# v of branch B: its load placed 14 products ahead of its transposes and splits

## The chip, the cores and the metric

One core of a Trainium2 chip runs the whole kernel. The metric is the device time of one execution in microseconds (us). Three runs of the kernel before gave 1984.55, 1987.9 and 1991.54 us; their median is 1987.9 us.

Names of the engines: PE is TensorE (matmuls and transposes), DVE is VectorE, ACT is ScalarE, POOL is GpSimd, and SP is SyncE, which here only issues transfers. POOL issues transfers too.

## The reference

One layer of a bidirectional encoder over 1024 tokens of width 1024, all in float32:

```python
h = x + 1/2 * SwiGLU_1(RMSNorm(x))
u = RMSNorm(h)
qa, ka, va, qb, kb, vb, ga, gb = split(u @ w_in)       # 512,512,512, 512,128,128, 1024,1024 columns
ya = neighbourhood_attention_2d(qa, ka, va, rpb)       # branch A: 8 heads of 64
yb = windowed_gqa_sink(rope(qb), rope(kb), vb, sink)   # branch B: 8 heads, 2 key/value heads of 64
h = h + (sigmoid(ga) * (ya @ w_a) + sigmoid(gb) * (yb @ w_b)) @ w_out
h = h + 1/2 * SwiGLU_2(RMSNorm(h))
y = RMSNorm_final(h)
```

The change is about `vb`, the 128 columns of the projection that are the values of branch B. They must be ready when branch B's attention begins, after the projection.

## The kernel before

**Exact products in three passes.** Every float32 operand is split into a high part (a copy to the rounded type `F32R`, made by ACT, line L88) and a low part (the rest, a subtraction made by DVE, L89). `mm3` multiplies high by high, high by low and low by high (L140, L142, L144). A matmul of 128x128 by 128x512 thus costs three.

**The projection as Strassen products.** The projection `u @ w_in` is run by `products` with `store_z`. It takes four channel blocks of 128 columns at a time, a "group" of two pairs (`m` = 0 and 1), and forms each pair with seven products of half size, P1, P2, P5, P6, P7, P3 and P4. So a group has 14 products, and there are five groups, 0 to 4: 70 products. One product is 12 matmuls on PE (4 chunks by 3 passes). While a product runs, ACT and DVE prepare the left sides of the products up to 8 later (`prep`, tiles `ws`), and ACT and DVE take the results out of the PSUM banks into slots of `fa` (`store_z`, L627 and L630). POOL then sends these to memory: `z_d` for the raw channels, `zs_d` for ready-made high and low parts (tiles `hs`), `g_d` for gates. The weights come through SP, one 512 KB tile at a time (`fetch`, L265, tiles `raw` or `fx`).

**PSUM.** There are eight banks, four with tag `g` and four with tag `d`. A group holds two `g` banks (its W sums, from P1 to P4) and, in turn, two and two `d` banks.

**What hangs on the products.** After given products, `at_end` calls what stands in `hooks` for the number of products that are still to come. `rope` (five times, k = 0 to 4) reads a block of q or k of branch B back from `z_d` in two shapes (tiles x and y, both from the pool `xs` of two buffers; L648 and L651, on SP), combines them on DVE (L652 to L654) and sends the result to `zr_d` (L655, on POOL). `v_b` reads block 17, the raw `vb`, back from `z_d` into one `xs` tile (L660), transposes it on PE in eight pieces into two `g` banks (L664), and splits these into the two tiles `mix["vb"]` (ACT L88 and DVE L89, four each, 128x256). `q_b`, `k_b` and `keep_u` follow at the end of the last group.

The hook of `v_b` has the number `14 * (NG - 2) - 12`, which is 30 products to come: it is called after P3 (m = 1) of group 2. That is the place in the program's text. The place in an engine's queue is chosen by a scheduler, which sorts the instructions of all engines before the kernel is built and keeps to the data; each engine then runs its own queue strictly in that order. PE, DVE, ACT, POOL and SP therefore each have a row of their own, and an instruction that waits holds up all that stand behind it on the same engine.

Of the kernel before, what the change touches and what calls it, by code (L numbers as in the profile page):

```python
# [15 lines left out]
P = 128  # L16
# [20 lines left out]
def trunk_kernel(ctx, tc, x, n1, wg1, wu1, wd1, nm, win, rpb, sink, wa, wb, wo,  # L37
                 n2, wg2, wu2, wd2, nf, c_rope, c_mask_a, c_mask_b, out):
    nc = tc.nc
# [10 lines left out]
    def nm_(s):  # L50
        uid[0] += 1
        return f"{s}_{uid[0]}"
# [11 lines left out]
    def new_fx(k, dt=F32):  # L64
        fx[k] = main.tile([P, 1024], dt, tag=f"fx{k}", bufs=1, name=nm_("fx"))
        return fx[k]
# [8 lines left out]
    def bank(tag):  # L75
        return ps.tile([P, 512], F32, tag=tag, name=nm_(tag))
# [4 lines left out]
    def xs4():  # L81
        return main.tile([P, 1024], F32, tag="xs", bufs=2, name=nm_("xs"))
# [4 lines left out]
    def split(dst_hi, dst_lo, src, eng=None):  # L87
        nc.scalar.copy(dst_hi, src)  # L88
        (eng or nc.vector).tensor_tensor(dst_lo, src, f32v(dst_hi), op=ALU.subtract)  # L89
# [492 lines left out]
    z_d = dram.tile([GA, T], F32, name="z_d")  # L582
# [8 lines left out]
    mix = {}  # L591
# [3 lines left out]
    NG = len(groups)  # L595
# [44 lines left out]
    def rope(k):  # L640
# [13 lines left out]
        nc.vector.tensor_tensor(x, x, y, op=ALU.add)  # L654
        nc.gpsimd.dma_start(zr_d[k], x)  # L655

    def v_b():
        mix["vb"] = [new_fx(k, F32R).rearrange("p (t d) -> p t d", t=NTT) for k in (0, 1)]
        r = xs4()
        nc.sync.dma_start(r, z_d[17 * P:18 * P, :])  # L660
        for n in range(2):
            pt = bank("g")
            for i in range(4):
                nc.tensor.transpose(pt[:, i * P:(i + 1) * P], r[:, (4 * n + i) * P:(4 * n + i + 1) * P], ident)  # L664
            pt = pt.rearrange("p (b s d) -> p b s d", s=2, d=HD)
            for s in range(2):
                v = mix["vb"][s][:, 4 * n:4 * n + 4, :]
                split(v[:, :, :HD], v[:, :, HD:], pt[:, :, s, :])
# [64 lines left out]
    def hook(n, *f):  # L733
        hooks.setdefault(n, []).append(f)

    for c in range(4):
        hook(14 * (NG - 1) - 2 - 3 * c, rope, c)
    hook(14 * (NG - 2) - 2, rope, 4)
    hook(14 * (NG - 2) - 12, v_b)
    hook(7, q_b, 0)  # L740
    hook(6, k_b)
    hook(4, q_b, 1)
# [357 lines left out]
    for i, dc in enumerate(a_order):  # L1100
        r = nxt.pop(0)
# [99 lines left out]
```

## Time and profile before

| what | value |
|---|---|
| runs | 1984.55, 1987.9, 1991.54 us, median 1987.9 |
| profiled execution | span 1987.6 us from its first to its last instruction; no other time of it is given |
| PE busy | 1938.4 us, 98% of the span |
| DVE, ACT, POOL busy | 1439.8, 957.4, 422.0 us |
| mean granted clock of PE | 0.993 of full speed |
| first matmul of the projection's group 3 | starts at 798.91 us of the span |

In a timeline's row the first number is the start in us from the span's start, the second the duration; then come engine, line, operation, out<-in and the count. A bracket gives the idle time before it and what ended that. A matmul's duration there is longer than its share of the engine, since matmuls overlap: the pace is read from start to start. In a row of a table by stretches the columns are the stretch, its length, the busy time (and the number of instructions) of PE, of PE's weight loads, of DVE, ACT and POOL, and then the granted clock of PE, the share of the DMA engines and GB/s. In a table of waits the numbers are the time in all, how often, and the longest.

### The profile page before, as it was taken

How to read it: one execution, taken by the hardware profiler on the slowest of the kernel's cores; microseconds unless marked ns; L12 is line 12 of the kernel's file. 1: busy time of each engine (PE TensorE's matmuls, PEld its weight loads, DVE VectorE, ACT ScalarE, POOL GpSimd, SP SyncE). 2: the span in 40 equal slices, each digit the busy share in tenths (PEclk: the TensorE clock that was granted, in tenths of full speed). 3: DMA queues.
4: the chain of work that ended last, by engine and by line, in shares of the span. 5: the costliest groups of instructions: out<-in, count | busy, mean ns of one | idle time of the engine just before them, and what ended most of it. 6: DMA issues, size and time to landing. Idle time of an engine off the chain costs nothing.

```text
span 1987.6 us, 25701 instructions
## 1 busy us (share of the span) xinstructions
PE 1938.4 (98%) x8968; PEld 1612.7 (81%) x8968; DVE 1439.8 (72%) x2495; ACT 957.4 (48%) x1857; POOL 422.0 (21%) x474
## 2 busy tenths in 40 slices
PE   6999999999999999999999999998999999999998
PEld 5788888888888778788888888887888888888886
DVE  7866566558967677768889866999656656659864
ACT  7433333334446443468777873365333333344453
POOL 4101001002500533311112134513101100105100
PEclk9999999999999999999999999999999999999999
DMA  6423323367233469973357675544332342393341
GB/s 194 147 85 106 121 92 106 108 220 277 84 121 125 145 160 243 201 174 107 87 143 173 172 253 195 179 147 127 120 114 88 105 126 85 125 349 129 108 140 62
DMA packets 257217, 290.31 MB, mean 146 GB/s; under 512 B 46880, under 2 KB 187552, under 8 KB 257088
## 3 DMA queue, kind: packets, MB, share of 16 engines
q1 hardware_dynamic: 200576, 203.09, 32.8%
q0 software_dynamic: 56512, 85.58, 15.2%
q8 instruction: 71, 1.16, 0.2%
q14 instruction: 58, 0.48, 0.1%
HBM read 202.01 MB, written 86.70 MB: 145 GB/s over the span
## 4 chain that ended last, share of the span: by engine, by line
PE 82%; DVE 8%; issue 4%; DMA 3%; POOL 2%; ACT 2%; SPq 0%; POOLq 0%; DVEq 0%; ACTq 0%
PE g L140 16%; PE g L142 16%; PE g L144 16%; PE d L140 10%; PE d L142 10%; PE d L144 10%; PE d L991 2%; DVE ws L89 2%; DVE ar L89 1%; DMA xs<-z_d 1%; PE d L970 1%; PE d L971 1%; PE g L1010 1%; PE g L1005 1%; DVE ar L1116 1%
## 5 line engine op out<-in xcount | busy, mean ns | idle before, releaser
L140 PE MATMUL g<-ar,ws 128*128 128x512 f32 x1208 | 455.7, 398 | 9.2 <-ACT ar L88 3.5
L142 PE MATMUL g<-ar,ws 128*128 128x512 f32 x1208 | 448.6, 392 | 3.7 <-DVE ar L89 3.7
L144 PE MATMUL g<-ar,ws 128*128 128x512 f32 x1208 | 447.3, 392 | 2.1 <-DVE ws L89 2.0
L89 DVE TENSOR_TENSOR ws<-raw,ws 128x512 fp32r<-128x512 f32 (+1 forms) x335 | 249.5, 748 | 189.6 <-ACT ws L88 188.4
L88 ACT CAST ws<-raw 128x512 fp32r<-128x512 f32 (+1 forms) x337 | 213.3, 638 | 272.6 <-PE d L144 108.5
L142 PEld LDWEIGHTS g<-ar,ws 128*128 128x128 f32 x1208 | 228.4, 189 | 52.0 <-DVE ar L89 4.4
L144 PEld LDWEIGHTS g<-ar,ws 128*128 128x128 f32 x1208 | 228.3, 189 | 51.7 <-DVE ws L89 3.2
L140 PEld LDWEIGHTS g<-ar,ws 128*128 128x128 f32 x1208 | 223.0, 189 | 51.9 <-ACT ar L88 4.7
L140 PE MATMUL d<-ar,ws 128*128 128x512 f32 x656 | 254.3, 392 | 4.7 <-DVE ar L89 4.7
L142 PE MATMUL d<-ar,ws 128*128 128x512 f32 x656 | 254.2, 391 | 0.0
L144 PE MATMUL d<-ar,ws 128*128 128x512 f32 x656 | 254.0, 391 | 0.0
L347 POOL DMA_DIRECT2D hid<-fx x98 | 53.1, 542 | 501.1 <-DVE fx L374 364.6
L140 PEld LDWEIGHTS d<-ar,ws 128*128 128x128 f32 x656 | 124.1, 189 | 31.4 <-issue 5.5
L144 PEld LDWEIGHTS d<-ar,ws 128*128 128x128 f32 x656 | 124.1, 189 | 25.9
L142 PEld LDWEIGHTS d<-ar,ws 128*128 128x128 f32 x656 | 124.0, 189 | 25.9
L89 DVE TENSOR_TENSOR ws<-ar,ws 128x512 fp32r<-128x512 f32 x114 | 109.1, 964 | 6.7 <-ACT ws L88 6.7
L89 DVE TENSOR_TENSOR ws<-fa,ws 128x512 fp32r<-128x512 f32 x80 | 55.3, 691 | 63.5 <-ACT ws L88 63.1
L88 ACT CAST ar<-raw 128x512 fp32r<-128x512 f32 (+1 forms) x83 | 56.0, 679 | 93.1 <-PE g L142 51.1
L140 PE MATMUL g<-ws,ws 128*128 128x512 f32 x232 | 90.9, 392 | 0.0
L142 PE MATMUL g<-ws,ws 128*128 128x512 f32 x232 | 90.4, 390 | 0.0
L144 PE MATMUL g<-ws,ws 128*128 128x512 f32 x232 | 90.3, 389 | 0.0
L978 ACT ACTIVATE fa<-fa,nmx 128x385 f32<-128x385 f32 (+3 forms) x128 | 75.5, 591 | 26.9 <-DVE nmx L975 26.2
(222 smaller groups left out, 3588.3 us busy)
## 6 DMA issues: line engine op xcount, KB each, us to landing
raw<-hid SPq DMA_DIRECT2D x70, 512.0 KB
hid<-fx POOLq DMA_DIRECT2D x98, 256.0 KB, 2.4
raw<-in_ffn_w_up_dram SPq DMA_DIRECT2D x32, 512.0 KB
ar<-in_ffn_w_down_dram SPq DMA_DIRECT2D x32, 512.0 KB
raw<-in_ffn_w_gate_dram SPq DMA_DIRECT2D x28, 512.0 KB
hid<-fa POOLq DMA_DIRECT2D x56, 256.0 KB, 2.7
raw<-in_w_in_dram SPq DMA_DIRECT2D x27, 512.0 KB
ar<-zs_d POOLq DMA_DIRECT2D x48, 256.0 KB, 5.0
```

Of the source, the lines that this page charges most:

```text
L88: nc.scalar.copy(dst_hi, src)
L89: (eng or nc.vector).tensor_tensor(dst_lo, src, f32v(dst_hi), op=ALU.subtract)
L140: nc.tensor.matmul(b, lhs[0], r[0], start=first, stop=False, **kw)
L142: nc.tensor.matmul(b, lhs[0], r[1], start=False, stop=False, **kw)
L144: nc.tensor.matmul(b, lhs[1], r[0], start=False, stop=last, **kw)
L347: nc.gpsimd.dma_start(hid[PRODUCTS.index(p), i], src)
L970: nc.tensor.matmul(b[:, :nw], un["q"][s], un["kd"][s][:, k0 * P:k1 * P], start=True, stop=False)
L971: nc.tensor.matmul(b[:, :nw], un["q"][s], un["kl"][s][:, k0 * P:k1 * P], start=False, stop=True)
L978: nc.scalar.activation(pr, pr, AF.Exp, scale=-1.0, bias=nmx[:, s:s + 1], accum_out=ssum[:, s:s + 1])
L991: nc.tensor.transpose(pt[:, i * P:(i + 1) * P], un["pr"][s][:, i * P:(i + 1) * P], ident)
L1005: nc.tensor.matmul(o[:, s], un["v"][s][:, un["k0"] + i, :], un["p"][s][:, i], start=i == 0, stop=i == last)
L1010: nc.tensor.matmul(o, un["v"][0][:, un["k0"] + i, :], un["p"][k][:, i], start=i + k == 0, stop=i + k == last + 1)
```

## The change

`v_b` is cut in two. `v_b_load` takes the `xs` tile and issues the load; it is hooked at 34 products to come, after P6 (m = 1) of group 2, four products earlier than before. `v_b` keeps the transposes and splits; it is hooked at 20 products to come, after P6 (m = 1) of group 3, ten products later than before.

```diff
+    def v_b_load():
+        mix["vraw"] = xs4()
+        nc.sync.dma_start(mix["vraw"], z_d[17 * P:18 * P, :])
+
     def v_b():
         mix["vb"] = [new_fx(k, F32R).rearrange("p (t d) -> p t d", t=NTT) for k in (0, 1)]
-        r = xs4()
-        nc.sync.dma_start(r, z_d[17 * P:18 * P, :])
+        r = mix.pop("vraw")
         for n in range(2):
             pt = bank("g")
...
     hook(14 * (NG - 2) - 2, rope, 4)
-    hook(14 * (NG - 2) - 12, v_b)
+    hook(14 * (NG - 2) - 8, v_b_load)
+    hook(14 * (NG - 2) - 22, v_b)
```

In the changed kernel the load is L659 and the transposes are L667. What the scheduler makes of it shows in the rows of three engines. In the names, `ws` is a left side of a product, `ar` a right side, `g` and `d` are PSUM banks, `xs` is the tile with the raw values.

PE before, at the transposes. The bank `d_6040` is P5 (m = 1) of group 3, `g_5941` is P1 (m = 0) of group 3:

```order
L142 MATMUL d_6040<-ar_4770,ws_5897 128x512
L144 MATMUL d_6040<-ar_4770,ws_5897 128x512
L664 MATMUL g_5877<-ident,xs_5875 128x128 [waits DMAHW4_49]
L664 MATMUL g_5877<-ident,xs_5875 128x128 x3
L664 MATMUL g_5886<-ident,xs_5875 128x128 x4
L140 MATMUL g_5941<-ar_4405,ws_5771 128x512 [waits Activation_49]
L142 MATMUL g_5941<-ar_4405,ws_5771 128x512
```

PE now, at the transposes. The bank `g_5938` is P6 (m = 1) of group 3, `g_5921` is P7 (m = 0) of it:

```order
L142 MATMUL g_5938<-ar_4769,ws_5918 128x512
L144 MATMUL g_5938<-ar_4769,ws_5918 128x512
L667 MATMUL g_6070<-ident,xs_5787 128x128 [waits DMAHW4_49,PE_49]
L667 MATMUL g_6070<-ident,xs_5787 128x128 x3
L667 MATMUL g_6079<-ident,xs_5787 128x128 [waits PE_49]
L667 MATMUL g_6079<-ident,xs_5787 128x128 x3
L140 MATMUL g_5921<-ar_84,ws_5935 128x512 [waits Activation_49]
```

Before, 45 matmuls of group 3 (P2, P2, P5 and nine of P5's last twelve) stood between group 2 and the transposes, and P1 of group 3 behind them. Now group 3 runs in its usual order, and 96 of its matmuls (P1, P2, P5, P6, two each) stand ahead of the transposes.

SP before, at the load. L651 is the last part of rope 4's loads, L265 a weight tile of group 4, L95 the weights of the first gate:

```order
L651 DMA xs_5662<-z_d 32x1024 x2
L660 DMA xs_5875<-z_d 128x1024 [waits DMAHW1_49,DMAHW0_49,DMAHW2_49,DMASW3_49,DMAHW3_49,DMASW2_49,DVE_49]
L265 DMA raw_6088<-in_w_in_dram 128x8x128 [waits DVE_49,Pool_49]
L95 DMA xs_6473<-in_w_in_dram 128x8x128 [waits DMAHW6_49,DMASW3_49]
L265 DMA raw_6090<-in_w_in_dram 128x8x128 [waits DMAHW7_49,DVE_49]
```

SP now, at the load:

```order
L651 DMA xs_5662<-z_d 32x1024 x2
L659 DMA xs_5787<-z_d 128x1024 [waits DMAHW1_49,DMAHW0_49,DMAHW2_49,DMASW3_49,DMAHW3_49,DMASW2_49,DVE_49]
L265 DMA raw_6088<-in_w_in_dram 128x8x128 [waits DVE_49,Pool_49]
L95 DMA xs_6473<-in_w_in_dram 128x8x128 [waits DMAHW6_49,DMASW3_49]
L265 DMA raw_6090<-in_w_in_dram 128x8x128 [waits DMAHW7_49,DVE_49]
```

Nothing moved there: the load stands at the same place among SP's 551 rows, with the same waits, the last of them on DVE.

ACT before, at the splits of v (`fx_5873` and `fx_5874`):

```order
L88 CAST ws_5996<-raw_5765 128x512
L627 COPY fa<-d_6023 128x512
L88 CAST fx_5873<-g_5877 128x4x64
L88 CAST fx_5873<-g_5886 128x4x64
L88 CAST fx_5874<-g_5877 128x4x64
L88 CAST fx_5874<-g_5886 128x4x64
L627 COPY fa<-g_5941 128x512
```

ACT now, at the splits of v (`fx_6068` and `fx_6069`; `g_5921` and `g_5938` are the sums of P6 of group 3, `ws_6092` is the left side of group 4's second P1):

```order
L627 COPY fa<-g_5921 128x512
L88 CAST ws_6052<-fx_77 128x512
L627 COPY fa<-g_5938 128x512
L88 CAST fx_6068<-g_6070 128x4x64
L88 CAST ws_6092<-raw_6088 128x512
L88 CAST fx_6068<-g_6079 128x4x64
L88 CAST fx_6069<-g_6070 128x4x64
L88 CAST fx_6069<-g_6079 128x4x64
```

The splits moved back behind the copies of P6's sums. On DVE the four subtractions moved back in the same way, from ahead of the copy of group 3's first P2 to ahead of that of its first P7. The rows of POOL stand as they stood, and apart from the stretch shown (some 100 rows of PE, 14 of DVE, 20 of ACT) so do all others. In PSUM, the transposes used to take the two banks that group 1 had left, so that group 3 took over group 2's; now group 3 takes the banks that group 1 left, the transposes take over group 2's, and group 4 takes over those of the transposes.

## The prediction

> **What bounds the kernel now.** I read the page first, then PE's waits, then PE's timeline at the transposes, and last the chain of waits to see what they hang on. From the page:
>
> ```profile
> span 1987.6 us, 25701 instructions
> PE 1938.4 (98%) x8968; PEld 1612.7 (81%) x8968; DVE 1439.8 (72%) x2495; ACT 957.4 (48%) x1857; POOL 422.0 (21%) x474
> PE 82%; DVE 8%; issue 4%; DMA 3%; POOL 2%; ACT 2%; SPq 0%; POOLq 0%; DVEq 0%; ACTq 0%
> ```
>
> PE is busy for 98% of the span and carries 82% of the chain that ended last. So what counts is where PE stands still, and at which clock it runs. PE's waits from 800 to 890 us hold one row, and its timeline shows the place (798.91 is the first matmul of group 3):
>
> ```profile
> PE g L664 <- DMA xs<-z_d: 4.5, 1, 4.5
> ...
> 798.91 0.39 PE L140 MATMUL d<-ar,ws 128*128 128x512 f32 x1
> ...
> 808.88 0.39 PE L144 MATMUL d<-ar,ws 128*128 128x512 f32 x1
> 813.79 1.97 PE L664 MATMUL g<-ident,xs 128*128 128x128 f32 x8 [4.51 <-DMA xs<-z_d]
> 815.41 0.78 PE L140 MATMUL g<-ar,ws 128*128 128x512 f32 x1
> 815.98 0.63 PE L142 MATMUL g<-ar,ws 128*128 128x512 f32 x1
> ...
> 818.54 0.47 PE L142 MATMUL g<-ar,ws 128*128 128x512 f32 x1
> 818.85 0.40 PE L144 MATMUL g<-ar,ws 128*128 128x512 f32 x1
> ```
>
> The transposes wait for their load, and all matmuls of group 3 behind them wait too. From 798.91 to 808.88 there are 44 steps: the pace is 0.2266 us a matmul. From 815.98 to 818.54 six steps take 2.56 us, 0.427 each. The table by stretches says why (the number before the last two is the granted clock):
>
> ```profile
> 808.00:812.00 4.00, 1.27 (x6) 0.73 (x4) 3.01 (x4) 0.38 (x1) 0.55 (x1) 0.98 0.27 71
> 812.00:816.00 4.00, 2.21 (x10) 2.12 (x11) 0.42 (x1) 0.58 (x2) 0.00 (x0) 0.50 0.99 328
> 816.00:820.00 4.00, 4.00 (x13) 3.17 (x12) 1.18 (x3) 0.83 (x4) 0.00 (x0) 0.66 0.46 134
> 820.00:824.00 4.00, 4.00 (x19) 3.33 (x18) 2.66 (x5) 3.01 (x6) 1.61 (x2) 1.00 0.17 42
> ```
>
> The idle PE lost half its clock, and ran at half speed till about 818.5. So the stall has a tail.
>
> What the load waited for stands in the chain of waits, with SP's rows behind it:
>
> ```profile
> 795.15 5.23 DMA zr_d<-xs
> ...
> 807.36 1.24 DVE xs L653
> 808.62 1.24 DVE xs L654
> 809.87 3.87 DMA xs<-z_d
> ```
> ```profile
> 809.87 0.34 SPq L660 DMA_DIRECT2D xs<-z_d  x1
> 811.12 0.40 SPq L265 DMA_DIRECT2D raw<-in_w_in_dram  x1
> ```
>
> The load was not late because it was issued at its use. It needed an `xs` buffer, and that became free when rope 4's addition (L654) ended at 809.86; SP issued it at 809.87, and it landed at 813.74. In front of that stand rope 3's store and rope 4's loads, a chain that PE's pace does not set at this point.
>
> **The change part by part.** *The load.* SP's row is unchanged, and so is the buffer and its release by L654. Nothing ahead of it on SP, POOL or DVE moved. On ACT the two copies of P1's sums come in earlier (0.59 us each, as in the row at 799.53 below, from about 801.6 on), ahead of P7's left sides, whose low parts stand before L653 on DVE; but L653 starts only with its data, at 807.36. So I cost the earlier hook at nothing: the load is still issued at 809.87 and lands at 813.74.
>
> *The transposes.* This is what moves. Ahead of them stand now 96 matmuls of group 3 and not 45. If PE runs through from 798.91, their turn comes at 798.91 + 96 x 0.2266 = 820.66, which is 6.9 us after the landing. The wait goes. Their own cost without a stall is seen at eight others of the same shape amid a full stream:
>
> ```profile
> 611.27 0.39 PE L144 MATMUL g<-ws,ws 128*128 128x512 f32 x1
> 611.50 1.03 PE L133 MATMUL d<-ident,xs 128*128 128x128 f32 x8
> 612.29 0.48 PE L140 MATMUL g<-ws,ws 128*128 128x512 f32 x1
> 612.61 0.39 PE L142 MATMUL g<-ws,ws 128*128 128x512 f32 x1
> ```
>
> From 611.27 to 612.61 are two matmul steps (0.45) and the transposes: 1.34 - 0.45 = 0.89 us.
>
> *The sum on PE.* Before, from 808.88 to 818.85, 9.97 us pass. In it are nine matmul steps, 9 x 0.2266 = 2.04 us, and eight transposes, worth 0.89 us at full clock. What is left is 9.97 - 2.04 - 0.89 = 7.04 us. Of this 4.68 us are the standstill (808.88 + 0.23 to 813.79), and 2.36 us the slow clock behind it.
>
> [...]
>
> *Group 3 in its usual order.* P1 comes ahead of P2 and P5 now. Its banks are those of group 1, long read. Are the left sides ready?
>
> ```profile
> 794.76 0.69 DVE L89 TENSOR_TENSOR ws<-raw,ws 128x512 fp32r<-128x512 f32 x1
> ...
> 804.60 0.69 DVE L89 TENSOR_TENSOR ws<-raw,ws 128x512 fp32r<-128x512 f32 x1
> ```
>
> The first is P2's second left side; P1's two stand ahead of it on DVE, so P1 finds them at 798.91. The second is that of P6 (m = 1), needed at 798.91 + 84 x 0.2266 = 817.9: 12 us of slack. I cost this at nothing. The cover is that preparation up to 8 products ahead; if it were gone, DVE would be late next.
>
> *The splits.* Four casts on ACT and four subtractions on DVE move as they are. Before, ACT stood still for them:
>
> ```profile
> 814.94 0.37 ACT L88 CAST fx<-g 128x256 fp32r<-128x256 f32 x1 [6.56 <-PE g L664]
> ...
> 816.20 1.29 DVE L89 TENSOR_TENSOR fx<-g,fx 128x256 fp32r<-128x256 f32 x3 [0.43 <-ACT fx L88]
> ```
>
> From the transposes' start to the last subtraction it was 817.49 - 813.79 = 3.7 us. Now they stand behind P6's copy, which ends just before the transposes, so ACT hardly waits. The work queued behind them is group 4's left sides.
>
> *Who waits for the banks.* The transposes take over group 2's banks; ACT's last copy out of them was this row:
>
> ```profile
> 799.53 0.59 ACT L627 COPY fa<-g 128x512 f32<-128x512 f32 x1
> ```
>
> That is 20 us ahead of them. Group 4's P1 takes the banks over from the transposes. It stands 72 matmuls later, at 820.66 + 0.89 + 72 x 0.2266 = 837.9. The splits should end at about 820.66 + 3.7 + 1.3 (one more left side between, 0.62 + 0.69) = 825.7. That is 12 us of slack: nothing.
>
> *Does the gain reach the end?* What follows:
>
> ```profile
> 814.00:890.00 76.00, 76.00 (x334) 63.08 (x333) 47.91 (x77) 40.80 (x70) 19.34 (x24) 0.97 0.84 174
> 890.00:1988.00 1098.00, 1078.39 (x5187) 904.24 (x5185) 815.72 (x1594) 567.82 (x1173) 222.79 (x255) 1.00 0.45 143
> ...
> 1340.00:1360.00 20.00, 17.19 (x78) 13.95 (x77) 19.09 (x25) 12.58 (x22) 11.02 (x9) 0.91 0.37 122
> ```
>
> PE has no idle time in the 76 us behind the stall, so an earlier PE stays earlier. What could hold it there is the load of the weights behind v's load on SP. It stays at 811.12, while PE comes 7 us sooner; but its user, group 4's second P1, stands at about 840.6. After 890 the queues of all engines are the same rows and hang on what PE has done, so they shift as one. One unknown is left: PE's later stalls may meet another phase of the clock. The worst is in 1340 to 1360, where 0.09 x 20 = 1.8 us go to it. That can vanish or double, so the bounds are 7.04 - 1.8 = 5.2 and 7.04 + 1.8 = 8.8 us. I take the middle, since nothing points to either side.
>
> Sum: the profiled span 1987.6 - 7.04 = 1980.6. The median of the runs lies 0.3 above the span, hence 1980.9 us, 0.35% less. What a measurement of this kernel can tell from no change is about 0.3%, or 6.0 us; the three runs lie within 3.6 us of their median. So even with the mechanism right, it is a close call.
>
> **The rivals.**
>
> *The wait comes along.* The load keeps its place behind rope 4, so its landing may be later than in this one profile. SP's waits from 690 to 905 show what such a delay can be:
>
> ```profile
> SPq L651 <- DMA zr_d<-xs: 22.0, 4, 7.4
> ...
> SPq L648 <- DMA z_d<-fa: 12.1, 1, 12.1
> ```
>
> The mean wait of L651 is 5.5 us, which the slack of 6.9 covers. One more of 12.1 would bring the landing to 825.8 and leave a stall of 5.2 us with its tail of 2.4. All but nothing is gained: 1987.9. A delay between these leaves a short stall without a tail, 1 to 4 us, and gives 1982 to 1985. Against it speaks that nothing of the rope chain moved.
>
> *The gain is taken back later.* An engine other than PE would have to bind after 824. DVE is busy for 816 of the 1098 us after 890, PE for 1078; DVE binds in single places, and those shift along. It gives 1986 to 1988.
>
> *Slower.* Group 4's P1 now needs the banks of the transposes. If ACT or DVE came to the splits late, held by a store that has not freed a slot of `fa`, PE would stop at 837.9. It decides when the splits end later than 837.9 + 7.0 = 844.9, 19 us after the 825.7 above; at 25 us late the price is 13 us, and the time 1987.9 - 7.0 + 13 = 1993.9. Before, group 4 took over the transposes' banks as well, and no wait showed there; only the distance was longer, 123 matmuls and not 72.
>
> [...]
>
> **How the numbers follow.** The stall goes as summed: 0.76, the rule on transposes within it (0.03). The wait comes along, in part or whole: 0.12. Taken back: 0.07. Slower: 0.05. Of the 0.76, run-to-run spread around -7.0 against the bound of -6.0 leaves about 0.58 beyond it and 0.18 inside; a short stall adds 0.02 beyond. So faster 0.60, within 0.35, slower 0.05. The likeliest case's own range is 1979.1 to 1982.7 by the bounds of the clock. To hold 8 in 10 with the spread of the runs and the short stalls I take 1977.5 to 1986.0.
>
> **What the profile after would show.** Right: the transposes have no wait, eight of them in about 1.0 us (not 1.97), at about 820.7; the clock is 1.00 from 796 to 836; v's load is still issued at about 809.9; group 4's P1 starts at about 837.9 without a wait; branch B's attention begins 7 us earlier, and the span is about 1980.6. Wrong: a wait for `xs<-z_d` at the transposes (the rope chain is later), a wait of PE for ACT or DVE at a product of group 3 or 4 (the preparation or the banks), or an unchanged span in spite of a stream without a gap (taken back).

## The result, and the profile after

The changed kernel took 1982.03 us (median of 10 runs, 1979.86 to 1983.76), the kernel before 1987.31 us in the same comparison (10 runs, 1984.01 to 1991.54). By the medians it is 5.3 us faster. The ratio is 0.9971, with a 95% interval of 0.9962 to 0.998: 0.29% faster, just inside the 0.3% that the prediction took as measurable, though the interval excludes no change. The runs also scatter less, over 3.9 us in place of 7.5.

The page of the changed kernel, with the share of the chain that ended last by engine in its third line:

```profile
span 1980.2 us, 25703 instructions
PE 1935.0 (98%) x8968; PEld 1609.3 (81%) x8968; DVE 1438.2 (73%) x2495; ACT 957.0 (48%) x1857; POOL 421.1 (21%) x474
PE 89%; DVE 4%; issue 2%; POOL 2%; DMA 1%; SPq 1%; ACT 1%; POOLq 0%; DVEq 0%; ACTq 0%
```

PE's share of the chain rose from 82 to 89%, DMA's fell from 3 to 1%: rope 3's store, rope 4 and v's load are no longer on it. PE's waits have no row for L667. Its timeline, with group 3's first matmul, the transposes, and the first matmul of the attention:

```profile
797.35 0.39 PE L140 MATMUL g<-ar,ws 128*128 128x512 f32 x1
...
818.88 0.39 PE L144 MATMUL g<-ar,ws 128*128 128x512 f32 x1
819.12 1.03 PE L667 MATMUL g<-ident,xs 128*128 128x128 f32 x8
819.91 0.48 PE L140 MATMUL g<-ar,ws 128*128 128x512 f32 x1
820.22 0.40 PE L142 MATMUL g<-ar,ws 128*128 128x512 f32 x1
...
874.40 0.28 PE L974 MATMUL d<-ar,ar 128*128 128x256 f32 x1
```

There is no bracket at L667, so no idle time, and eight transposes take 1.03 us, not 1.97. From 818.88 to 820.22 are two matmul steps (0.45) and the transposes: 0.89 us. The table by stretches, over the time in which PE stood and then ran slow before:

```profile
808.00:812.00 4.00, 4.00 (x19) 3.33 (x18) 3.63 (x6) 2.61 (x5) 2.30 (x4) 1.00 0.92 279
812.00:816.00 4.00, 4.00 (x20) 3.30 (x19) 1.39 (x2) 1.36 (x3) 1.24 (x2) 1.00 2.19 287
816.00:820.00 4.00, 4.00 (x24) 3.40 (x23) 1.39 (x2) 1.79 (x4) 0.00 (x0) 1.00 1.67 278
...
814.00:883.00 69.00, 68.98 (x315) 57.05 (x314) 45.36 (x78) 38.21 (x67) 15.86 (x20) 1.00 0.93 183
```

PE is busy throughout, and the granted clock, 0.98, 0.50 and 0.66 in these three stretches before, is 1.00. The load in SP's timeline, with the weight tile behind it, and the end of the splits on DVE:

```profile
807.27 0.34 SPq L659 DMA_DIRECT2D xs<-z_d  x1
809.12 0.40 SPq L265 DMA_DIRECT2D raw<-in_w_in_dram  x1
```
```profile
821.34 0.75 DVE L89 TENSOR_TENSOR fx<-g,fx 128x256 fp32r<-128x256 f32 x2
822.52 0.43 DVE L89 TENSOR_TENSOR fx<-g,fx 128x256 fp32r<-128x256 f32 x1 [0.44 <-ACT fx L88]
```

In this execution group 3 begins at 797.35, 1.56 us earlier than in the profile of before, so the transposes' turn, 820.66 as forecast, came at 819.12. The first matmul of the attention stood here in the profile of before:

```profile
883.02 0.28 PE L970 MATMUL d<-ar,ar 128*128 128x256 f32 x1
```

It moved from 883.02 to 874.40, 8.62 us, of which 1.56 were there already: 7.06 us come from this place.

### The profile page after: what moved, and what is told of

Its sections match the earlier page's. It is cut to its first block, busy times and chain, and to the rows that moved or that the text cites. A ratio compares the mean times of both kernels' runs of the same rounds, so it can differ in the third digit from the quotient of the medians.

```text
span 1980.2 us, 25703 instructions
## 1 busy us (share of the span) xinstructions
PE 1935.0 (98%) x8968; PEld 1609.3 (81%) x8968; DVE 1438.2 (73%) x2495; ACT 957.0 (48%) x1857; POOL 421.1 (21%) x474
## 4 chain that ended last, share of the span: by engine, by line
PE 89%; DVE 4%; issue 2%; POOL 2%; DMA 1%; SPq 1%; ACT 1%; POOLq 0%; DVEq 0%; ACTq 0%
PE g L140 17%; PE g L142 17%; PE g L144 17%; PE d L140 11%; PE d L142 11%; PE d L144 11%; PE d L995 2%; DVE ws L89 1%; PE d L974 1%; PE d L975 1%; PE g L1009 1%; PE g L1014 1%; DVE ar L89 1%; POOL ar L89 1%; PE d L133 0%
```

## The experiments

The theory: what counts is how many of PE's matmuls stand between the start of group 3 and the transposes, against the time at which v's load lands; the load's hook does nothing, because a buffer sets the load's time. The rivals: the earlier load is what helps; the transposes' place helps through something else (the order of group 3, the banks); or the load lands early enough anyway and the tail is what counts.

**The load alone.** The load at its new hook, transposes and splits at the old one:

```diff
-    hook(14 * (NG - 2) - 22, v_b)
+    hook(14 * (NG - 2) - 12, v_b)
```

> Only the load's hook is moved (34 products to come); the transposes keep the place of before. The rows of all five engines come out as those of before. Theory (what counts is where the transposes stand on PE, behind or ahead of the landing; the load itself waits for rope 4's buffer): no change, ratio to before 0.999 to 1.001, a wait of 3.5 to 4.8 us for the load at the transposes, a half clock behind it. Rival (the earlier hook of the load brings the gain): ratio about 0.997, no wait.

1988.43 us (12 runs) against 1988.66 of before (24 runs), ratio 1.0 [0.9992, 1.0008]. The rows of all five engines are those of before. The stall is back, in PE's timeline and in the table by stretches:

```profile
809.14 0.39 PE L144 MATMUL d<-ar,ws 128*128 128x512 f32 x1
815.77 1.97 PE L667 MATMUL g<-ident,xs 128*128 128x128 f32 x8 [6.24 <-DMA xs<-z_d]
```
```profile
812.00:816.00 4.00, 0.23 (x1) 0.24 (x2) 0.77 (x2) 0.00 (x0) 0.42 (x1) 0.77 0.85 253
816.00:820.00 4.00, 4.00 (x14) 3.52 (x14) 1.61 (x4) 1.39 (x4) 0.00 (x0) 0.50 0.87 258
```

The earlier hook is worth nothing. The wait was longer than expected, 6.24 us: with the same rows as before it varies from one execution to the next.

**The transposes alone.** The kernel before, load and transposes together at the new late hook:

```diff
-    hook(14 * (NG - 2) - 12, v_b)
+    hook(14 * (NG - 2) - 22, v_b)
```

> Only the hook of the whole v_b is moved back to 20 products to come, with its load directly at the transposes as before. The rows of all five engines come out as those of the changed kernel. Theory (place of the transposes): the whole gain, ratio 0.996 to 0.998, no wait at the transposes, load issued about 10 to 11 us after the first matmul of group 3 as in both kernels. Rival (the load must stand ahead): the load comes too late, ratio 1.000 or above.

1982.3 us (5 runs), ratio 0.9965 [0.9952, 0.9978]. All rows are those of the changed kernel, the load's on SP too, although its hook stands 14 products later. The load in SP's timeline, and the transposes in PE's, without a wait:

```profile
809.45 0.34 SPq L660 DMA_DIRECT2D xs<-z_d  x1
```
```profile
820.01 1.04 PE L664 MATMUL g<-ident,xs 128*128 128x128 f32 x8
```

This half of the change is the whole of it.

**48 matmuls ahead.** The changed kernel with the transposes four products earlier, so that group 3 keeps its usual order and the banks are as after, but 48 of its matmuls stand ahead in place of 96:

```diff
-    hook(14 * (NG - 2) - 22, v_b)
+    hook(14 * (NG - 2) - 18, v_b)
```

> The transposes are hooked at 24 products to come: group 3 runs in its usual order (P1 first, banks as in the changed kernel), but only 48 matmuls stand ahead of the transposes (45 before, 96 in the changed kernel). Theory: the landing decides. The turn comes 48 x 0.2266 = 10.9 us after group 3's first matmul, the landing 13.8 (profile after) to 14.8 us (profile before) after it: a wait of 2.9 to 3.9 us with a tail of 0 to 2.4, so ratio 0.998 to 1.000. Rival (the usual order of group 3 and its banks bring the gain, not the distance to the landing): no wait, ratio 0.997.

1987.99 us (11 runs, 1982.8 to 1991.96), ratio 0.9991 [0.9981, 1.0001]. So neither the order of group 3 nor the banks make the gain. But the profiled execution, one of 1984.1 us, had a wait without a slow clock, a little under the 2.9 to 3.9 us expected:

```profile
811.24 1.06 PE L667 MATMUL g<-ident,xs 128*128 128x128 f32 x8 [2.81 <-DMA xs<-z_d]
```
```profile
812.00:816.00 4.00, 4.00 (x20) 3.33 (x19) 2.21 (x5) 2.63 (x7) 1.72 (x2) 1.00 1.69 315
```

Four more single executions of the same kernel ask what its wide scatter is:

> The kernel with the transposes at 24 products to come once more, for another profile. Its timed runs lay between 1982.8 and 1992.0 us, and its profile (a run of 1984.1 us) had a wait of 2.8 us without a fall of the clock. If a fall of the clock that comes in some executions only makes the spread, a run above 1986 shows a wait of 3 to 5 us and a half clock behind it, and a run below 1985 shows none. If the clock stays at 1.00 there in a slow run too, the spread comes from elsewhere.

> The same a third time: half clock behind the wait if the run is above 1986 us, none if below 1985.

> The same kernel as the one with 48 matmuls ahead, once more, for one question: its runs scatter from 1982 to 1992 us, and the three profiled ones (1984.1, 1982.4, 1985.9) had waits of 2.8, 1.8 and 3.0 us without a slow clock behind them. If the scatter is the length of the wait (landing against PE) with a tail beyond some 4 us, then a run of 1988 us or more shows a wait above 3.5 us and a granted clock under 1.00 behind it, and one under 1986 shows neither. If the scatter has another place in the kernel, a run of 1988 us or more shows a wait of 1.8 to 3.0 us here and the clock at 1.00, and the loss stands elsewhere.

> As for the look before it: over 1988 us, a wait above 3.5 us and a clock under 1.00 behind it by the one theory, a wait of at most 3.0 us at clock 1.00 by the other; under 1986 us, no tail by both.

They took 1982.41, 1985.85, 1988.31 and 1988.49 us; the kernel before took 1989.69 beside the first two and 1989.02 beside the last two, one run each. The transposes of the four in PE's timeline:

```profile
810.38 1.06 PE L667 MATMUL g<-ident,xs 128*128 128x128 f32 x8 [1.82 <-DMA xs<-z_d]
```
```profile
811.66 1.06 PE L667 MATMUL g<-ident,xs 128*128 128x128 f32 x8 [2.97 <-DMA xs<-z_d]
```
```profile
813.74 1.79 PE L667 MATMUL g<-ident,xs 128*128 128x128 f32 x8 [5.05 <-DMA xs<-z_d]
```
```profile
814.69 1.74 PE L667 MATMUL g<-ident,xs 128*128 128x128 f32 x8 [4.73 <-DMA xs<-z_d]
```

And the stretches of the third of them, where the clock falls as in the kernel before, though for a shorter time:

```profile
812.00:816.00 4.00, 2.26 (x10) 2.20 (x11) 2.19 (x5) 1.29 (x4) 1.65 (x2) 0.74 1.06 330
816.00:820.00 4.00, 4.00 (x16) 3.20 (x16) 1.42 (x4) 1.37 (x4) 1.72 (x2) 0.84 1.66 313
```

The same rows give a wait of 1.8 to 5.05 us. Up to 2.97 the clock stays at 1.00; at 4.73 and 5.05 it falls, to means of 0.71 and 0.74 over the lowest stretch of 4 us. The last two could have gone against this, and did not: both were over 1988 us, and both have the long wait and the slow clock. The second, 1985.85 us, fell between the two bounds that were set for it.

**60 matmuls ahead**, one product later than that:

```diff
-    hook(14 * (NG - 2) - 22, v_b)
+    hook(14 * (NG - 2) - 19, v_b)
```

> The transposes are hooked at 23 products to come: 60 matmuls of group 3 ahead of them. Theory: the turn comes 13.6 us after group 3's first matmul, the landing at 13.8 to 14.8: a wait of 0 to 1.2 us, too short for the clock to fall, so nearly the whole gain: ratio 0.9965 to 0.998. If the tail of 2.4 us also follows a short wait, ratio about 0.998 to 0.999.

1982.72 us (6 runs), ratio 0.997 [0.9959, 0.9981]: the timed gain is all but that of 96.

```profile
808.23 0.34 SPq L659 DMA_DIRECT2D xs<-z_d  x1
```
```profile
812.60 1.06 PE L667 MATMUL g<-ident,xs 128*128 128x128 f32 x8 [1.23 <-ACT fa L627]
```

A wait of 1.23 us is left, without a slow clock (1.00 in every stretch of 4 us from 796 to 836). The bracket names ACT, but ACT's last copy out of the transposes' banks had ended by 798.4, 14 us earlier; the load had been issued 4.37 us before. It was the load: ACT had long been done with these banks, and in the profiled execution of 1984.1 us, with 48 ahead, the load took 3.89 us from its issue at 807.21 to its landing.

**The load twice, and three times.** The changed kernel, with the line of the load repeated; the later copies write the same values again, and so move only the landing:

```diff
         nc.sync.dma_start(mix["vraw"], z_d[17 * P:18 * P, :])
+        nc.sync.dma_start(mix["vraw"], z_d[17 * P:18 * P, :])
```

The other kernel has the new line twice.

> The changed kernel with v's load issued twice into the same tile, the second behind the first's landing; the rows of PE, DVE, ACT and POOL are those of the changed kernel. Theory: what counts is the slack between landing and turn, 6.9 us by the profile before and about 8 by the profile after. The second load lands 3.9 to 4.4 us later, 17.7 to 19.2 us after group 3's first matmul; the turn is at 21.75: still no wait, ratio to before 0.996 to 0.998, as the changed kernel. Rival (the gain hangs on the load's time itself): about 4 us of the gain go, ratio 0.998 to 0.999.

> The same with the load issued three times. Theory: the third lands 22 to 23.6 us after group 3's first matmul, just behind the turn at 21.75: a wait of 0.3 to 1.9 us without a fall of the clock, ratio 0.9965 to 0.9985, and the wait seen in the profile. Rival (each load costs its 4 us): ratio 1.000.

Twice took 1983.14 us (9 runs), ratio 0.9977 [0.9967, 0.9987] against 1988.53 of before (24 runs); three times 1991.57 (10 runs), ratio 1.0017 [1.0008, 1.0027]. Twice, on SP and on PE:

```profile
809.87 0.34 SPq L659 DMA_DIRECT2D xs<-z_d  x1
813.81 0.33 SPq L660 DMA_DIRECT2D xs<-z_d  x1
```
```profile
820.74 1.03 PE L668 MATMUL g<-ident,xs 128*128 128x128 f32 x8
```

Three times:

```profile
807.10 0.34 SPq L659 DMA_DIRECT2D xs<-z_d  x1
811.12 0.33 SPq L660 DMA_DIRECT2D xs<-z_d  x1
817.03 0.38 SPq L661 DMA_DIRECT2D xs<-z_d  x1
```
```profile
824.87 1.94 PE L669 MATMUL g<-ident,xs 128*128 128x128 f32 x8 [5.77 <-DMA xs<-z_d]
```

A landing some 4 us later costs nothing, so the slack is real. A landing that passes the transposes' turn brings back the whole loss and more. The size was missed: I expected a wait of 0.3 to 1.9 us and a ratio of at most 0.9985, by copies of 3.9 to 4.4 us each. From row to row the first copy took 4.0 us, the second 5.9, and the third 7.8 (to the transposes' start). The rival's 1.000 is nearer to the measured 1.0017, but that each copy costs its 4 us is ruled out by the kernel with two. The copies also hold up what stands behind them on SP (the first load of `zr_d` is issued at 817.51 with three, at 814.35 in the profile of the changed kernel); that was not separated, but little is left for it: 1983.14 us without a wait and the 8.23 us that the table below has as lost here make 1991.4.

**The buffer.** The kernel before, with rope 4's second tile taken from the pool of left sides, so that v's load need not wait for L654:

```diff
-        x, y = xs4(), xs4()
+        x, y = xs4(), spare_xs() if k == 4 else xs4()
```

> The kernel before with rope 4's second tile (y) in a buffer of the pool of left sides, so that v's load no longer waits for rope 4's addition but for rope 3's store, 9 us sooner (800.4 and not 809.9 in the profile before). The scheduler now sets the transposes 2 matmuls ahead of group 3's first, 47 matmuls sooner than before. Theory (the scheduler sets the transposes where it believes that the load lands, and on the chip the rope chain is later than it believes): the load lands 5 to 6 us after group 3 would begin, the transposes wait 4 to 7 us with a tail, ratio 0.999 to 1.001. Rival (the buffer alone was the cause, so that with it free the wait is gone): no wait, ratio 0.996 to 0.998.

1990.67 us (10 runs), ratio 1.0014 [1.0002, 1.0025]. The load was issued 10 us sooner, and the wait stood there all the same:

```profile
799.71 0.34 SPq L660 DMA_DIRECT2D xs<-z_d  x1
```
```profile
803.31 1.97 PE L664 MATMUL g<-ident,xs 128*128 128x128 f32 x8 [5.31 <-DMA xs<-z_d]
```

So the buffer did set the load's time. But the transposes moved forward too in PE's queue, by 47 matmuls: they stand 2 matmuls ahead of group 3's first, in place of 45 behind it. That fits a scheduler which places them where it takes the load to have landed, and takes it to be some 5 us too early both times; that this is how it decides was not shown apart.

**Before, once more**, for the spread of its wait:

> The kernel before, unchanged, for another profile of its wait. Theory: the wait depends on how PE and the rope chain happen to stand to each other in an execution: between 2.5 and 6.5 us (4.5 in the profile before), its tail from none to 2.7 us; the load is issued at the end of rope 4's addition in each.

1989.21 us, with a wait of

```profile
813.69 1.97 PE L664 MATMUL g<-ident,xs 128*128 128x128 f32 x8 [4.19 <-DMA xs<-z_d]
```

**All profiled executions together.** "Lost" is worked out from PE's timeline as in the prediction's sum: from the last matmul ahead of the transposes to a matmul at full pace behind them, less 0.2266 us a step and 0.89 us for the transposes. "Matmuls ahead" counts those of group 3; -2 means that two of group 2 still stand behind the transposes.

| kernel | matmuls ahead | wait | lost | lost less wait | span | span less lost |
|---|---|---|---|---|---|---|
| 48 ahead | 48 | 1.82 | 2.04 | 0.2 | 1980.6 | 1978.6 |
| 48 ahead | 48 | 2.81 | 3.02 | 0.2 | 1982.3 | 1979.3 |
| 48 ahead | 48 | 2.97 | 3.18 | 0.2 | 1984.1 | 1980.9 |
| 60 ahead | 60 | 1.23 | 1.44 | 0.2 | 1981.1 | 1979.7 |
| before, again | 45 | 4.19 | 6.78 | 2.6 | 1987.4 | 1980.6 |
| before | 45 | 4.51 | 7.06 | 2.6 | 1987.6 | 1980.5 |
| 48 ahead | 48 | 4.73 | 6.57 | 1.8 | 1986.7 | 1980.1 |
| 48 ahead | 48 | 5.05 | 6.90 | 1.9 | 1986.5 | 1979.6 |
| buffer elsewhere | -2 | 5.31 | 7.44 | 2.1 | 1988.8 | 1981.4 |
| load three times | 96 | 5.77 | 8.23 | 2.5 | 1989.3 | 1981.1 |
| load alone | 45 | 6.24 | 8.92 | 2.7 | 1989.5 | 1980.6 |
| after | 96 | 0 | 0 | 0 | 1980.2 | 1980.2 |
| load twice | 96 | 0 | 0 | 0 | 1981.3 | 1981.3 |
| transposes alone | 96 | 0 | 0 | 0 | 1984.3 | 1984.3 |

Whatever was edited, the span less what was lost at this one place is 1978.6 to 1981.4 us, but for one execution (1984.3), of which 1.7 us are waits of PE at the attention's start (below) and 1.4 us come from one wait of PE for DVE (L1115) that took 1.7 us there and 0.3 us in the profile after. The place explains most of what sets these executions apart.

## Why the prediction was right

It said 1980.9 us, in 1977.5 to 1986.0; it was 1982.03. The mechanism was as forecast; of the two sides of the bound of 0.3%, which it had called a close call, the ratio came out on the less likely one, at 0.29% in place of 0.35%.

- *The load is still issued at L654's end, whatever its hook.* Right: the load alone kept the rows of before, and the transposes alone issued the load from the same row. The forecast time, 809.87, held to within 3.7 us: 806.2 to 811.6 in the profiles with the buffer of before. That spread of rope 4's chain against PE is what the prediction had seen only once.
- *The transposes come 6.9 us after the landing.* Right in kind and about in size. Of the executions whose transposes waited for the single load in before's buffer (before twice, the load alone, 48 ahead five times, 60 ahead), the start of the transposes less that of group 3 gives the landing 12.9 to 16.6 us behind group 3's start; the turn stands 21.75 behind it. The slack is thus 5.1 to 8.9 us.
- *The wait and its tail are worth 7.04 us.* Right for the profile that it was read from: 7.06 us came free between group 3 and the attention. The same wait measured by single executions of before's order is 6.78 to 8.92 us lost, and by timed runs 5.3 us in the first comparison, 6.4 in the next (transposes alone against before, 1988.66 less 1982.3). So the profile that the forecast was read from had lost more than the median run of before.
- *The tail of 2.36 us.* Right here, but it comes with long waits alone. Counted as in the prediction's sum, behind the standstill, it is nothing at waits of 2.97 us and less and 1.7 to 2.5 us at 4.19 and more; the column "lost less wait" holds some 0.2 us besides. Counted from where PE stopped, the clock of the profile before fell after 2.6 us by the estimate in the last section. The two executions with 48 ahead and a slow clock show a tail of 1.7 us, the others 2.0 to 2.5.
- *The sum against the median.* This is the term that was mis-sized. I put the median 0.3 us above the span, by before's three runs and its span. In the runs after, each time stands 1.8 us above its own span (1981.98 and 1980.2 for the profiled one), so that the profiled execution of before was one of some 1989.4 us, slower than its median. The forecast span, 1980.6, was 0.4 from the measured one; 1980.6 + 1.8 = 1982.4 would have been 0.4 from the median. That the span came so near holds some luck: group 3 began 1.56 us earlier in the profile after, and 1.2 us were lost again behind the attention's first matmul (below).
- *Group 3's usual order, the splits and the banks cost nothing.* Right: no wait of PE from 814 to 883. The splits ended at 822.95, 3.8 us after the transposes' start, where I had allowed 5.0; group 4's P1, 72 matmuls behind the transposes, found its banks free with some 13 us to spare. The rival by which it would be slower was far off.
- *The wait comes along.* It did not, in the three profiles with 96 ahead and the load once or twice. The load three times shows its price: 8.23 us lost for a wait of 5.77, where I had 7.6 for one of 5.2. Short stalls without a tail, which I had put at 1 to 4 us, were seen at waits of 1.23 to 2.97 us; a wait of 4.19 us had a tail. The time, 1991.57 in place of 1987.9, is further off, but the kernel before took 1988.53 in that comparison, and 1983.14 + 8.23 is 1991.4.
- *Taken back later.* In small part. In the profile after the attention's first matmul came 8.62 us sooner, and the span ended 7.4 us sooner (1987.6 less 1980.2): 1.2 us went behind that matmul, and where was not traced. In three others PE waits again at the start of the attention's stretch: 1.7 us in all with the transposes alone, 1.0 us in the third execution with 48 ahead, and 0.5 us with the load three times. The table by stretches of the first of these, from 830 to 900, where the profile after has PE busy for 69.98 of 70:

```profile
830.00:900.00 70.00, 68.34 (x322) 56.54 (x321) 46.84 (x106) 42.04 (x84) 14.22 (x20) 1.00 0.77 165
```

  PE's timeline there names `ar`, a right side of its products:

```profile
883.50 0.50 PE L140 MATMUL g<-ar,ws 128*128 128x512 f32 x1 [0.91 <-ACT ar L88]
884.76 0.50 PE L142 MATMUL g<-ar,ws 128*128 128x512 f32 x1 [0.53 <-DVE ar L89]
```

  So an execution can give back a quarter of the gain there; I had put all of 7 us or none on this rival.
- *The 0.03 for a rule on transposes.* No run shows such a rule. In the profile after, the eight transposes took 0.89 us amid a full stream, and the granted clock was 1.00 from 816 to 824.

## What to carry to other kernels

Where PE waits for a load, first ask what releases the load: if it is a buffer, an earlier hook moves nothing (here 1988.43 us against 1988.66), and it is the consumer that has to move. Put it behind the landing as the chip shows it, with a slack that covers the landing's spread (here 3.7 us between executions), and check the place that a scheduler has chosen against that. The waits of PE behind which the clock fell cost more here than their length, so halving such a wait may give more than half: with 48 ahead, waits of 1.82 to 2.97 us lost 2.0 to 3.2 us, and waits of 4.73 and 5.05 us lost 6.6 and 6.9. A time that is compared with one profile should be that profile's own and not the median.

## What the runs showed of the hardware

- At this place the clock fell in the long waits and not in the short ones. Five executions of one and the same kernel lost 2.04, 3.02 and 3.18 us for waits of 1.82, 2.81 and 2.97 us, with a clock of 1.00 in every stretch of 4 us from 804 to 824, but 6.57 and 6.90 for 4.73 and 5.05, with clocks of 0.86 and 0.71, and of 0.74 and 0.84, from 812 to 816 and 816 to 820: some 2 us more of waiting cost 3.4 to 3.7. No profiled execution has a wait at this place between 2.97 and 4.19 us.
- The length of the wait alone does not decide it. An estimate: if the clock is either 1.00 or 0.50, the lowest that a stretch shows, a stretch of 4 us has 4 x (1 - clock) / 0.5 us at half clock. Before, that makes 0.16, 4 and 2.72 us from 808 to 820: the clock fell at 811.84, 2.6 us after PE had stopped (813.79 less the wait of 4.51, so 809.28), and was low for 6.9 us. With 48 ahead and a wait of 5.05 us it makes 2.08 and 1.28 us: the clock fell at 813.92, 5.2 us after PE had stopped (813.74 less 5.05, so 808.69) and just after it had begun again, and was low for 3.4 us. Yet the waits of 2.81 and 2.97 us passed without a fall. What else decides was not shown; the part of the low time that falls into the wait costs nothing, so the tail differs as well.
- Kernels with this wait mostly scatter more: 7.5, 8.1 and 9.2 us (before, the load alone, 48 ahead), against 3.9 and 2.7 without it (after, the load twice). It is not clean: the load three times has 5.7 with the wait, the transposes alone 5.1 without it, by one long run of five.
- One and the same 512 KB load took 4.0 us, 5.9 and 7.8 from row to row when issued three times in a row. In SP's timeline one load of weights was issued during the first, two during the second, and two of `zr_d` during the third. So the 4.0 us that the load took with one other beside it were no bound here for the same load among more.
